# A decoder trunk with its five engines in program order, weight splits two tiles ahead

## The chip, the cores and the metric

The kernel runs on one core of one Trainium2 chip, in one launch. Its time is the device time of that core in microseconds (us), the median of several runs. Five engines work side by side and meet at semaphores: TensorE (PE) multiplies matrices, VectorE (DVE), ScalarE (ACT) and GpSimd (POOL) work element by element, SyncE (SP) issues transfers. Each takes its own instructions in the order in which they are written into its program.

## The reference, cut to what matters

Two layers over 256 tokens of width 1024, in float32, then a final RMSNorm:

```python
h = rmsnorm(x, norm_mix[l])
p = h @ w_in[l]
a_x, a_c, a_b, q, k, v, g, z, gates = split(p)
y_a = short_conv_mixer(a_x, a_c, a_b, conv_w[l]) @ w_a_out[l]
r = retention(rotary(q), rotary(k), v, ret_gn[l])
y_b = (silu(g) * r) @ w_b_out[l]
y_c = spatial_gating(gelu(z), sg_ln[l], sg_w[l], sg_b[l]) @ w_c_out[l]
g_a, g_b, g_c = split(sigmoid(gates), 3)
x = x + (g_a * y_a + g_b * y_b + g_c * y_c) @ w_o[l]
h = rmsnorm(x, norm_xa[l]); mm = rmsnorm(mem, norm_mem[l])
x = x + cross_attention(h, mm, xa_q[l], xa_k[l], xa_v[l], xa_o[l])   # 4 heads of 256
h = rmsnorm(x, norm_ffn[l])
x = x + (silu(h @ w1[l]) * (h @ w3[l])) @ w2[l]                       # width 2816
```

## The kernel before

Activations lie transposed in SBUF (features on the partitions, 256 tokens along the free side), so a product with a weight takes K tiles of 128 features. To come near float32 with TensorE's fp32r type, every operand is a pair hi + lo, where hi is the value rounded to fp32r and lo the rest, and a product is three: hi·hi, hi·lo and lo·hi. On PE a K tile of 128x128 weights is one matmul of hi against [x hi, x lo] (512 columns) and one of lo against x hi (256 columns).

All weights form one stream, `ws`, of 320 tiles of 128x1024 (512 KB), in the order in which PE wants them. A tile of most stages holds four K tiles of 256 output columns, so a chunk of 256 columns over K = 1024 takes two tiles. `fetch()` does three things with a tile: it issues the transfer into `raw` (five buffers) on SP's queue, lets ACT round it to `hi` (line 106) and DVE subtract to `lo` (both four buffers). `weights()` hands PE the next columns and calls `fetch()` for AHEAD = 1 tile ahead.

The stages of a layer: q/k and v together, z, g, then ax, ac, ab (the convolution's factors), twelve chunks of gates (gt), the three branches' outputs (y) with their gated merge (ye, mg), the first quarter of the keys (k), wo, the other keys, q, the values (xv) with the four heads' attention between (s, pT, av), xo, the FFN's f chunks, w2. In wo, xo and w2 every chunk ends in `residual()`, which adds the PSUM chunk to `xT` in two DVE additions, and `prepare()`, which splits the new `xT` into `xs` for the next stage (ACT makes the hi part with the gain, DVE the lo part, for two blocks) and lets POOL square and sum it into an accumulator (sq, acc). For gates and f chunks the sum of the two PSUM halves is made by `summed()` (a copy by ACT, an addition by DVE), gated by DVE or POOL with the row of norms (rb), and passed on. A gate chunk goes on to ACT's sigmoid into gs. During the gates, the memory tokens (`m2`, from `memT`) are loaded, squared (first layer), scaled on POOL and split into `mmt` for the keys.

What sets the order: only PE's instructions are bound to the order in which the program writes them, by the class `InOrder` (line 36), which gives every instruction a dependency on the one before it on that engine. Those of DVE, ACT, POOL and SP are placed by the framework's scheduler, which runs a timeline model of its own when the program is built, and may take a later tile's split ahead of a written earlier instruction.

Of the kernel before, what the change touches and what calls it, by code (L numbers as in the profile page):

```python
# [17 lines left out]
P = 128  # L18
# [8 lines left out]
LAYER_COLS = 163840  # L27
NPAR = 48
WARM = 9
AHEAD = 1  # L30

IN = dict(ax=0, ac=256, ab=512, q=768, k=1024, v=1280, g=1792, z=2304, gates=2816)

# [20 lines left out]
@with_exitstack  # L54
def decoder_trunk(ctx: ExitStack, tc: tile.TileContext, a, out):
    nc = tc.nc
    V, A, G, T = nc.vector, nc.scalar, nc.gpsimd, InOrder(tc, nc.tensor)

    const = ctx.enter_context(tc.tile_pool(name="const", bufs=1))
    res = ctx.enter_context(tc.tile_pool(name="res", bufs=1))  # L60
# [5 lines left out]
    def tt(e, o, x, y, op):  # L66
        e.tensor_tensor(o, x, y, op=op)  # L67
# [18 lines left out]
        at = sum(m for _, _, m in pieces[-1])  # L86
        pieces[-1].append((at, c, n))
    assert len(pieces) == tiles
    state = dict(pos=0, loaded=0)
    ready = []  # L90
    later = []

    def fetch():
        n = state["loaded"]
        if n == tiles:
            return
        state["loaded"] = n + 1
        raw = wts.tile([P, TW], F32, tag="raw", name=f"raw{n}", bufs=5)
        hi = wts.tile([P, TW], F32R, tag="hi", name=f"hi{n}", bufs=4)
        lo = wts.tile([P, TW], F32R, tag="lo", name=f"lo{n}", bufs=4)  # L100
        for at, c, m in pieces[n]:
            nc.sync.dma_start(raw[:, at:at + m], ws[c // TW, :, c % TW:c % TW + m])
        w = TW if n else TW // 2
        for c in range(0, TW, w):
            sl = slice(c, c + w)
            A.activation(hi[:, sl], raw[:, sl], AF.Copy)  # L106
            tt(V, lo[:, sl], raw[:, sl], f32(hi[:, sl]), ALU.subtract)
        if n >= 4 and later:
            later.pop(0)()
        ready.append((hi, lo))  # L110

    def weights(cols):
        pos = state["pos"]
        while state["loaded"] <= min(pos // TW + AHEAD, tiles - 1):
            fetch()
        o = pos % TW
        state["pos"] = pos + cols
        hi, lo = ready[pos // TW]
        return hi[:, o:o + cols], lo[:, o:o + cols]


    def chunk_T(xs, kt, name, hooks=None, ps=None, ks=None):


# [12 lines left out]
        return ps  # L137
# [85 lines left out]
    sgg = const.tile([P, L, 256], F32, name="sgg")  # L223
    gfin = const.tile([P, KT], F32, name="gfin")
    for t, n in ((cs, "cs"), (dec, "dec"), (tril, "tril"), (gfin, "gfin")):
        later.append(lambda t=t, n=n: nc.sync.dma_start(t, a[n]))
    later.append(lambda: nc.sync.dma_start(sgg, a["sgg"].partition_broadcast(P)))

    def param(l, name):
        o, n = dict(g_mix=(0, 8), g_xa=(8, 8), g_mem=(16, 8), g_ffn=(24, 8), gn=(32, 4),  # L230
# [50 lines left out]
    def new_acc(name):  # L281
        return wrk.tile([P, S], F32, tag="acc", name=name, bufs=2)
# [14 lines left out]

    acc = new_acc("acc0")
    for j in range(4):
        nc.sync.dma_start(xT[:, 2 * j:2 * j + 2], a["xT"][:, 2 * j:2 * j + 2])  # L300
        prepare(j, acc, param(0, "g_mix"))
        for _ in range((2, 1, 1, 0)[j]):
            fetch()
    rm = const.tile([P, S], F32, name="rm")

    for l in range(L):
# [38 lines left out]


        wm = wrk.tile([P, 4, P], F32, tag="wm", name="wm", bufs=1)
        nc.sync.dma_start(wm, a["wsT"][:, l])
        tt(G, wm, wm, mid(tril, 4), ALU.mult)
        st6 = wrk.tile([P, 2, 6], F32, tag="st6", name="st6")  # L350
        mv2 = wrk.tile([P, 2, 2], F32, tag="mv2", name="mv2")
# [50 lines left out]
        for i in range(2):
            V.tensor_scalar_mul(yc[:, i], zp[:, i, 2:], cw[:, 4 + i:5 + i])
            V.scalar_tensor_tensor(yc[:, i], zp[:, i, 1:S + 1], cw[:, 2 + i:3 + i], yc[:, i], ALU.mult, ALU.add)
            V.scalar_tensor_tensor(yc[:, i], zp[:, i, 0:S], cw[:, i:i + 1], yc[:, i], ALU.mult, ALU.add)
# [20 lines left out]
        for b in range(2):  # L426
# [4 lines left out]
            rv = rr[:, b].rearrange("p h d -> p (h d)")  # L431
            tt(G, rv, rv, sg[:, b], ALU.mult)

        tb = summed(chunk_T(of(xs), KT, f"ab{l}"))
        tt(G, tb, tb, mid(rb, 2), ALU.mult)
        tt(G, yc, yc, tb, ALU.mult)
        split(mo[:, 0:2], yc)
        split(mo[:, 6:8], transposes(su, 0, f"suT{l}"))


# [1 line left out]
        for c in range(12):  # L442
            t = summed(chunk_T(of(xs), KT, f"gt{l}_{c}"))
            tt(V, t, t, mid(rb, 2), ALU.mult)
            A.activation(gs[:, 2 * c:2 * c + 2], t, AF.Sigmoid)
            if c == 2 and l == 0:
                macc = new_acc("macc")
                for j in range(4):
                    m2 = wrk.tile([P, 2, S], F32, tag="pp", name="m2", bufs=2)
                    nc.sync.dma_start(m2, a["memT"][:, 2 * j:2 * j + 2])  # L450
                    add_squares(macc, m2, j == 0)
            if c == 5 and l == 0:
                rm_n = rstd_cols([macc], "rm_n")
# [32 lines left out]
        kv = wrk.tile([P, 8, 2, S], F32R, tag="A", name=f"kT{l}", bufs=1)
# [129 lines left out]
        if l + 1 < L:
# [114 lines left out]
```

## Time and profile before

| | |
|---|---|
| runs | 968.21, 968.31, 970.08 us; median 968.31 |
| the profiled execution | 969.4 us |
| its span (first to last instruction) | 967.6 us |
| mean granted clock of PE | 0.995 |
| instructions | 14606 |
| moved by DMA | 175.53 MB, 181 GB/s in the mean |

The span is 1.8 us shorter than the execution's time. "Busy" is the sum of an engine's instructions; a wait is put down to the semaphore that came last. The granted clock is PE's, 1.00 being full speed. Tile names in a row stand for all tiles of that name.

### The profile page before, as it was taken

How to read it: one execution, taken by the hardware profiler on the slowest of the kernel's cores; microseconds unless marked ns; L12 is line 12 of the kernel's file. 1: busy time of each engine (PE TensorE's matmuls, PEld its weight loads, DVE VectorE, ACT ScalarE, POOL GpSimd, SP SyncE). 2: the span in 40 equal slices, each digit the busy share in tenths (PEclk: the TensorE clock that was granted, in tenths of full speed). 3: DMA queues.
4: the chain of work that ended last, by engine and by line, in shares of the span. 5: the costliest groups of instructions: out<-in, count | busy, mean ns of one | idle time of the engine just before them, and what ended most of it. 6: DMA issues, size and time to landing. Idle time of an engine off the chain costs nothing.

```text
span 967.6 us, 14606 instructions
## 1 busy us (share of the span) xinstructions
PE 951.8 (98%) x5622; PEld 836.8 (86%) x5622; DVE 713.7 (74%) x884; ACT 539.8 (56%) x740; POOL 296.1 (31%) x232
## 2 busy tenths in 40 slices
PE   8999999999999999999999989999999999999996
PEld 6788889888998888888888878998889888888886
DVE  7679789886768866657655896799776778666654
ACT  6565765565645755654456465545665466656431
POOL 5943021320114644432134230024100345444211
PEclk9999999999999999999999999999999999999998
DMA  9664665555546565555656355555644556556541
GB/s 310 245 228 145 192 203 186 190 182 170 172 133 194 177 198 191 193 187 180 197 179 194 111 180 193 195 179 172 196 153 151 154 187 191 187 194 194 180 151 44
DMA packets 52630, 175.53 MB, mean 181 GB/s; under 512 B 6096, under 2 KB 6608, under 8 KB 52560
## 3 DMA queue, kind: packets, MB, share of 16 engines
q1 hardware_dynamic: 52128, 174.03, 55.9%
q8 instruction: 44, 0.72, 0.3%
q10 hardware_dynamic: 432, 0.57, 0.2%
q14 instruction: 26, 0.21, 0.1%
HBM read 173.53 MB, written 1.05 MB: 180 GB/s over the span
## 4 chain that ended last, share of the span: by engine, by line
PE 96%; DVE 2%; DMA 1%; issue 0%; SPq 0%; ACT 0%; DVEq 0%
PE f L43 25%; PE gt L43 14%; PE w L43 13%; PE y L43 5%; PE k L43 5%; PE xo L43 5%; PE wo L43 5%; PE xv L43 5%; PE q L43 5%; PE z L43 2%; PE g L43 2%; PE v L43 2%; PE qk L43 2%; PE av L43 1%; PE ac L43 1%; PE s L43 1%
## 5 line engine op out<-in xcount | busy, mean ns | idle before, releaser
L67 DVE TENSOR_TENSOR lo<-raw,hi 128x1024 fp32r<-128x1024 f32 (+1 forms) x321 | 436.8, 1363 | 200.0 <-ACT hi L106 198.0
L106 ACT ACTIVATE hi<-raw 128x1024 fp32r<-128x1024 f32 (+1 forms) x321 | 338.9, 1057 | 315.1 <-issue 67.5
L43 PE MATMUL f<-xs,hi 128*128 128x512 f32 x704 | 245.2, 393 | 0.0
L43 PE MATMUL f<-xs,lo 128*128 128x256 f32 x704 | 196.1, 279 | 0.0
L43 PEld LDWEIGHTS f<-xs,hi 128*128 128x128 f32 x704 | 131.9, 187 | 30.1 <-issue 0.4
L43 PE MATMUL gt<-xs,hi 128*128 128x512 f32 x384 | 136.5, 400 | 2.8 <-DVE ev L67 2.7
L43 PEld LDWEIGHTS f<-xs,lo 128*128 128x128 f32 x704 | 132.6, 188 | 0.0
L67 POOL TENSOR_TENSOR sq<-xT 128x512 f32<-128x512 f32 x27 | 45.8, 1695 | 239.3 <-DVE xT L67 234.5
L43 PE MATMUL gt<-xs,lo 128*128 128x256 f32 x384 | 107.8, 281 | 0.0
L67 POOL TENSOR_TENSOR ev<-ev,rb_ffn 128x512 f32<-128x512 f32 x44 | 63.8, 1453 | 108.3 <-DVE ev L67 85.3
L43 PEld LDWEIGHTS gt<-xs,hi 128*128 128x128 f32 x384 | 72.7, 189 | 20.6 <-DVE ev L67 4.0
L43 PEld LDWEIGHTS gt<-xs,lo 128*128 128x128 f32 x384 | 73.2, 191 | 0.0
L43 PE MATMUL w<-aB,hi 128*128 128x512 f32 (+1 forms) x198 | 62.7, 372 | 0.0
L43 PE MATMUL w<-aA,hi 128*128 128x512 f32 (+1 forms) x198 | 62.3, 371 | 0.0
L67 POOL TENSOR_TENSOR ev<-ev 128x256 f32<-128x256 f32 x44 | 50.5, 1151 | 20.1 <-ACT ev L597 20.1
L202 DVE SCALAR_TENSOR_TENSOR xs<-xT,par,xs 128x256 fp32r<-128x256 f32 x48 | 49.1, 1062 | 4.2 <-ACT xs L201 4.2
L43 PE MATMUL w<-aB,lo 128*128 128x256 f32 x176 | 49.5, 281 | 0.0
L43 PE MATMUL w<-aA,lo 128*128 128x256 f32 x176 | 49.4, 281 | 0.0
L43 PE MATMUL y<-mo,hi 128*128 128x256 f32 x256 | 46.1, 283 | 0.0
L43 PE MATMUL k<-mmt,hi 128*128 128x512 f32 x128 | 45.6, 400 | 0.0
L43 PE MATMUL q<-xs,hi 128*128 128x512 f32 x128 | 45.5, 398 | 0.0
L43 PE MATMUL xo<-ox,hi 128*128 128x512 f32 x128 | 45.4, 399 | 0.0
(251 smaller groups left out, 1779.9 us busy)
## 6 DMA issues: line engine op xcount, KB each, us to landing
raw<-in_ws SPq DMA_DIRECT2D x304, 512.0 KB, 3.5
raw<-in_ws SPq DMA_DIRECT2D x32, 256.0 KB, 4.0
m<-in_memT SPq DMA_DIRECT2D x12, 256.0 KB, 4.0
xT<-in_xT SPq DMA_DIRECT2D x4, 256.0 KB, 5.2
dec<-in_dec SPq DMA_DIRECT2D x1, 512.0 KB, 6.0
wm<-in_wsT SPq DMA_DIRECT2D x2, 256.0 KB, 4.8
out<-xT ACTq DMA_DIRECT2D x2, 256.0 KB, 2.3
sgg<-in_sgg SPq DMA_DIRECT2D x1, 256.0 KB, 5.1
```

Source lines behind the costliest of these rows:

```text
L43: ins = getattr(self.engine, name)(*args, **kwargs)
L67: e.tensor_tensor(o, x, y, op=op)
L106: A.activation(hi[:, sl], raw[:, sl], AF.Copy)
L202: V.scalar_tensor_tensor(lo, x, scale, f32(hi), ALU.mult, ALU.subtract)
```

## The change

All five engines become `InOrder`, so no scheduler moves an instruction. The program itself is written as a pipeline instead. `fetch()` is cut in two: `load()` issues the transfer and runs LOADED = 4 tiles ahead of the split, `cut()` makes hi and lo and is called when PE begins the tile AHEAD = 2 before. Work that waits for a POOL result is handed to `after(units, fn)`, which lets `weights()` call it so many K tiles (UNIT = 256 columns) later: the convolution's taps (3), its split (6), the memory's split (7), the merge of the branches (2), the FFN's gate (4) and hidden split (6). The memory tokens' squares are spread over gate chunks 2 to 5, and the tokens scaled in chunks 7 to 10 in place of 6 to 9. At the start all blocks of x and the first five weight tiles are issued to SP before the first `prepare()`. The computation is the same.

```diff
-AHEAD = 1
+AHEAD = 2
+LOADED = 4
+UNIT = 256
-    V, A, G, T = nc.vector, nc.scalar, nc.gpsimd, InOrder(tc, nc.tensor)
+    V, A, G, T, Y = (InOrder(tc, e) for e in (nc.vector, nc.scalar, nc.gpsimd, nc.tensor, nc.sync))
-    def fetch():
-        n = state["loaded"]
...
+    def load():
+        n = len(raws)
...
+        for at, c, m in pieces[n]:
+            Y.dma_start(raw[:, at:at + m], ws[c // TW, :, c % TW:c % TW + m])
+        raws.append(raw)
+    def cut():
+        n = len(ready)
...
+        while len(raws) <= n:
+            load()
...
+        if n >= 4:
+            while len(raws) <= min(n + LOADED, tiles - 1):
+                load()
...
+    def after(units, fn):
+        due.append((state["unit"] + units, fn))
     def weights(cols):
         pos = state["pos"]
-        while state["loaded"] <= min(pos // TW + AHEAD, tiles - 1):
-            fetch()
+        while len(ready) <= min(pos // TW + AHEAD, tiles - 1):
+            cut()
...
+        state["unit"] = pos // UNIT
+        for item in [d for d in due if d[0] <= state["unit"]]:
+            due.remove(item)
+            item[1]()
...
+                def memory(j=j, m2=m2):
+                    for n in range(2):
+                        split(mmt[:, 2 * j + n], m2[:, n], param(l, "g_mem")[:, 2 * j + n:2 * j + n + 1])
+                after(7, memory)
...
-            tt(V, ev[0], ev[0], ev[2], ALU.add)
-            split(mg[:, 2 * c:2 * c + 2], ev[0])
+            def merge(c=c, ev=ev):
+                tt(V, ev[0], ev[0], ev[2], ALU.add)
+                split(mg[:, 2 * c:2 * c + 2], ev[0])
+            after(2, merge)
...
-            A.activation(t[:, 0], t[:, 0], AF.Silu)
-            tt(G, t[:, 0], t[:, 0], t[:, 1], ALU.mult)
-            split(hidden(c), t[:, 0])
+            def gate():
+                A.activation(t[:, 0], t[:, 0], AF.Silu)
+                tt(G, t[:, 0], t[:, 0], t[:, 1], ALU.mult)
+            after(4, gate)
+            after(6, lambda: split(hidden(c), t[:, 0]))
```

In order rows, `lo60` is weight tile 60's lo part and the number behind an underscore tells two buffers apart; wo0_1 is layer 0's second chunk of wo. First DVE in wo of the first layer. Before:

```order
L67 TENSOR_TENSOR lo60_1864<-raw60_1862,hi60_1863 128x1024
L67 TENSOR_TENSOR kT0_1733<-ev_1779,kT0_1733 128x2x256
L67 TENSOR_TENSOR xT_73<-wo0_0_1785,xT_73 128x512 x2
L67 TENSOR_TENSOR lo61_1897<-raw61_1895,hi61_1896 128x1024
L202 SCALAR_TENSOR_TENSOR xs_74<-xT_73,par_75,xs_74 128x256 x2
L67 TENSOR_TENSOR lo62_1919<-raw62_1917,hi62_1918 128x1024
L67 TENSOR_TENSOR xT_73<-wo0_1_1839,xT_73 128x512 x2
L67 TENSOR_TENSOR lo63_1952<-raw63_1950,hi63_1951 128x1024
L202 SCALAR_TENSOR_TENSOR xs_74<-xT_73,par_75,xs_74 128x256 x2
```

After, DVE there reads:

```order
L45 TENSOR_TENSOR lo58_1801<-raw58_1676,hi58_1800 128x1024
L45 TENSOR_TENSOR lo59_1823<-raw59_1712,hi59_1822 128x1024
L45 TENSOR_TENSOR xT_73<-wo0_0_1799,xT_73 128x512 x2
L45 SCALAR_TENSOR_TENSOR xs_74<-xT_73,par_75,xs_74 128x256 x2
L45 TENSOR_TENSOR lo60_1855<-raw60_1750,hi60_1854 128x1024
L45 TENSOR_TENSOR lo61_1877<-raw61_1775,hi61_1876 128x1024
L45 TENSOR_TENSOR xT_73<-wo0_1_1853,xT_73 128x512 x2
L45 SCALAR_TENSOR_TENSOR xs_74<-xT_73,par_75,xs_74 128x256 x2
```

Between the additions to xT and the two operations on xs stood one split, and stands none; at wo's first addition the splits are done up to tile 60 before, up to tile 59 after.

DVE in xo of the first layer, whose first two chunks end one weight tile apart. Before:

```order
L67 TENSOR_TENSOR xT_73<-xo0_0_2737,xT_73 128x512 x2
L67 TENSOR_TENSOR lo92_2887<-raw92_2885,hi92_2886 128x1024
L202 SCALAR_TENSOR_TENSOR xs_74<-xT_73,par_75,xs_74 128x256 x2
L67 TENSOR_TENSOR xT_73<-xo0_1_2775,xT_73 128x512
L67 TENSOR_TENSOR lo93_2920<-raw93_2918,hi93_2919 128x1024
L67 TENSOR_TENSOR xT_73<-xo0_1_2775,xT_73 128x512
L67 TENSOR_TENSOR lo94_2942<-raw94_2940,hi94_2941 128x1024
L202 SCALAR_TENSOR_TENSOR xs_74<-xT_73,par_75,xs_74 128x256 x2
```

After:

```order
L45 TENSOR_TENSOR lo90_2814<-raw90_2663,hi90_2813 128x1024
L45 TENSOR_TENSOR xT_73<-xo0_0_2751,xT_73 128x512 x2
L45 SCALAR_TENSOR_TENSOR xs_74<-xT_73,par_75,xs_74 128x256 x2
L45 TENSOR_TENSOR lo91_2845<-raw91_2708,hi91_2844 128x1024
L45 TENSOR_TENSOR xT_73<-xo0_1_2789,xT_73 128x512 x2
L45 SCALAR_TENSOR_TENSOR xs_74<-xT_73,par_75,xs_74 128x256 x2
L45 TENSOR_TENSOR lo92_2878<-raw92_2756,hi92_2877 128x1024
```

Before, splits 92, 93 and 94 stand ahead of the second chunk's xs; after, only split 91 does, and both chunks' xT and xs are ahead of split 92.

ACT at the gates of the second layer, where m2_5769 and m2_5826 are pieces of the memory tokens and gt1_1 is the second gate chunk. Before:

```order
L190 ACTIVATE ev_5331<-gt1_0_5286 128x512
L198 ACTIVATE mo1_4686<-mixb1_4684 128x2x256
L106 ACTIVATE hi188_5428<-raw188_5427 128x1024
L106 ACTIVATE hi189_5456<-raw189_5455 128x1024
L190 ACTIVATE ev_5381<-gt1_1_5336 128x512
L201 ACTIVATE mo1_4686<-rT10_5386,par_75 128x256
L201 ACTIVATE mmt1_5654<-m2_5769,par_75 128x256 x2
L201 ACTIVATE mo1_4686<-rT12_5395,par_75 128x256
L445 ACT_TABLE_LOAD
L445 ACTIVATE gs1_5285<-ev_5331 128x512
L201 ACTIVATE mmt1_5654<-m2_5826,par_75 128x256 x2
L106 ACTIVATE hi190_5478<-raw190_5477 128x1024
```

After, the first piece of the memory tokens (m2_5719) comes here:

```order
L45 ACTIVATE ev_5663<-gt1_6_5618 128x512
L45 ACTIVATE gs1_5297<-ev_5663 128x512
L45 ACTIVATE hi198_5670<-raw198_5573 128x1024
L45 ACTIVATE hi199_5692<-raw199_5595 128x1024
L45 ACTIVATE ev_5714<-gt1_7_5669 128x512
L45 ACTIVATE gs1_5297<-ev_5714 128x512
L45 ACTIVATE hi200_5723<-raw200_5623 128x1024
L45 ACTIVATE hi201_5745<-raw201_5645 128x1024
L45 ACTIVATE mmt1_5668<-m2_5719,par_75 128x256 x2
```

The splits of the memory tokens stood among those of the first two gate chunks; they now stand behind the eighth gate chunk's sigmoid.

## Rows read from the trace of the kernel before

**Rows 1.** The page's busy time: us, share of span, instructions of each engine.

```profile
PE 951.8 (98%) x5622; PEld 836.8 (86%) x5622; DVE 713.7 (74%) x884; ACT 539.8 (56%) x740; POOL 296.1 (31%) x232
```

**Rows 2.** The chain that ended last: start, us, engine, tile, line, instructions.

```profile
91.22 22.19 PE gt L43 x128
147.36 23.03 PE y L43 x192
176.04 22.62 PE wo L43 x128
```

**Rows 3.** PE's waits: releaser, us in total, times, longest us.

```profile
PE gt L43 <- DVE ev L67: 2.7, 3, 2.1
PE qk L43 <- DVE lo L67: 2.0, 3, 0.7
PE rb_fin L43 <- DVE rn_fin L259: 1.3, 1, 1.3
PE qk L43 <- ACT hi L106: 0.9, 1, 0.9
PE rb_mix_ps L43 <- DVE rn_mix L259: 0.7, 1, 0.7
```

**Rows 4.** Timeline, second layer's gates: start, us, engine, line, operation, tile [idle before].

```profile
564.44 4.93 POOL L67 TENSOR_TENSOR m<-m,rm 128x512 f32<-128x512 f32 x2 [4.19 <-DMA m<-in_memT]
568.13 0.91 ACT L201 ACTIVATE mmt<-m,par 128x256 fp32r<-128x256 f32 x2 [3.69 <-POOL m L67]
577.19 0.50 PE L43 MATMUL gt<-xs,hi 128*128 128x512 f32 x1 [2.11 <-DVE ev L67]
```

**Rows 5.** Windows: the start, and behind that wait: busy us, clock, DMA share, GB/s.

```profile
5.50:32.00 26.50, 23.24 (x99) 17.72 (x100) 21.71 (x24) 15.25 (x22) 17.81 (x17) 1.00 1.00 352
578.40:581.90 3.50, 3.50 (x14) 2.94 (x13) 2.90 (x4) 0.97 (x2) 0.00 (x0) 0.51 0.78 256
```

**Rows 6.** Timeline of DVE, ACT and POOL in wo, first layer.

```profile
181.74 1.42 DVE L67 TENSOR_TENSOR xT<-wo,xT 128x512 f32<-128x512 f32 x2
183.07 1.22 DVE L67 TENSOR_TENSOR lo<-raw,hi 128x1024 fp32r<-128x1024 f32 x1
183.19 0.91 ACT L201 ACTIVATE xs<-xT,par 128x256 fp32r<-128x256 f32 x2 [0.46 <-DVE xT L67]
183.24 1.95 POOL L67 TENSOR_TENSOR sq<-xT 128x512 f32<-128x512 f32 x1 [11.05 <-DVE xT L67]
184.20 2.14 DVE L202 SCALAR_TENSOR_TENSOR xs<-xT,par,xs 128x256 fp32r<-128x256 f32 x2
186.27 1.21 DVE L67 TENSOR_TENSOR lo<-raw,hi 128x1024 fp32r<-128x1024 f32 x1
187.41 1.41 DVE L67 TENSOR_TENSOR xT<-wo,xT 128x512 f32<-128x512 f32 x2
191.93 1.76 DVE L67 TENSOR_TENSOR lo<-raw,hi 128x1024 fp32r<-128x1024 f32 x1
```

**Rows 7.** Groups by form: busy us, mean ns | idle before us and releaser.

```profile
L202 DVE SCALAR_TENSOR_TENSOR xs<-xT,par,xs 128x256 fp32r<-128x256 f32 x48 | 49.1, 1062 | 4.2 <-ACT xs L201 4.2
L198 ACT ACTIVATE mg<-ye 128x512 fp32r<-128x512 f32 x8 | 5.0, 628 | 0.8 <-DVE ye L67 0.7
L523 DVE TENSOR_REDUCE mx<-s 128x2 f32<-128x512 f32 x8 | 5.5, 684 | 0.0
L528 ACT ACTIVATE pp<-s,mx,rs 128x256 f32<-128x256 f32 x16 | 8.8, 557 | 5.5 <-DVE mx L67 5.5
L530 DVE RECIPROCAL sm<-sm 128x2 f32<-128x2 f32 x8 | 1.3, 164 | 9.2 <-ACT pp L528 9.2
```

**Rows 8.** Timeline: the same operation on m, POOL idle, second layer.

```profile
571.77 0.89 DVE L202 SCALAR_TENSOR_TENSOR mmt<-m,par,mmt 128x256 fp32r<-128x256 f32 x2 [0.73 <-ACT mmt L201]
```

**Rows 9.** Timeline: DVE in the y stage, first layer.

```profile
164.57 0.68 DVE L67 TENSOR_TENSOR mg<-ye,mg 128x512 fp32r<-128x512 f32 x1
165.17 0.68 DVE L67 TENSOR_TENSOR ye<-y,gs 128x512 f32<-128x512 f32 x1
```

More of the change, by code (lines that the diff above doesn't have):

```diff
@@ L88, in decoder_trunk @@
     assert len(pieces) == tiles
-    state = dict(pos=0, loaded=0)
-    ready = []
-    later = []
-    def fetch():
-        n = state["loaded"]
+    state = dict(pos=0, loaded=0, unit=0)
+    raws, ready = [], []
+    later, due = [], []
+    def load():
+        n = len(raws)
         if n == tiles:
             return
-        state["loaded"] = n + 1
         raw = wts.tile([P, TW], F32, tag="raw", name=f"raw{n}", bufs=5)
+        for at, c, m in pieces[n]:
[3 more added lines that the diff above has]
+        n = len(ready)
+        if n == tiles:
+            return
+        while len(raws) <= n:
+            load()
+        raw = raws[n]
         hi = wts.tile([P, TW], F32R, tag="hi", name=f"hi{n}", bufs=4)
         lo = wts.tile([P, TW], F32R, tag="lo", name=f"lo{n}", bufs=4)
-        for at, c, m in pieces[n]:
-            nc.sync.dma_start(raw[:, at:at + m], ws[c // TW, :, c % TW:c % TW + m])
         w = TW if n else TW // 2
@@ L107, in fetch @@
             tt(V, lo[:, sl], raw[:, sl], f32(hi[:, sl]), ALU.subtract)
-        if n >= 4 and later:
-            later.pop(0)()
         ready.append((hi, lo))
+        if n >= 4:
+            while len(raws) <= min(n + LOADED, tiles - 1):
+                load()
+            if later:
+                later.pop(0)()
+    def after(units, fn):
+        due.append((state["unit"] + units, fn))
     def weights(cols):
         pos = state["pos"]
-        while state["loaded"] <= min(pos // TW + AHEAD, tiles - 1):
-            fetch()
+        while len(ready) <= min(pos // TW + AHEAD, tiles - 1):
+            cut()
         o = pos % TW
         state["pos"] = pos + cols
+        state["unit"] = pos // UNIT
+        for item in [d for d in due if d[0] <= state["unit"]]:
+            due.remove(item)
+            item[1]()
         hi, lo = ready[pos // TW]
@@ L225, in decoder_trunk @@
     for t, n in ((cs, "cs"), (dec, "dec"), (tril, "tril"), (gfin, "gfin")):
-        later.append(lambda t=t, n=n: nc.sync.dma_start(t, a[n]))
-    later.append(lambda: nc.sync.dma_start(sgg, a["sgg"].partition_broadcast(P)))
+        later.append(lambda t=t, n=n: Y.dma_start(t, a[n]))
+    later.append(lambda: Y.dma_start(sgg, a["sgg"].partition_broadcast(P)))
     def param(l, name):
@@ L299, in decoder_trunk @@
     for j in range(4):
-        nc.sync.dma_start(xT[:, 2 * j:2 * j + 2], a["xT"][:, 2 * j:2 * j + 2])
+        Y.dma_start(xT[:, 2 * j:2 * j + 2], a["xT"][:, 2 * j:2 * j + 2])
+        for _ in range((2, 1, 1, 1)[j]):
+            load()
+    for j in range(4):
         prepare(j, acc, param(0, "g_mix"))
         for _ in range((2, 1, 1, 0)[j]):
-            fetch()
+            cut()
     rm = const.tile([P, S], F32, name="rm")
@@ L347, in decoder_trunk @@
         wm = wrk.tile([P, 4, P], F32, tag="wm", name="wm", bufs=1)
-        nc.sync.dma_start(wm, a["wsT"][:, l])
+        Y.dma_start(wm, a["wsT"][:, l])
         tt(G, wm, wm, mid(tril, 4), ALU.mult)
@@ L401, in decoder_trunk, with taps @@
         cw = param(l, "conv")
[L402 to L405, printed above, removed]
+        def taps():
+            for i in range(2):
+                V.tensor_scalar_mul(yc[:, i], zp[:, i, 2:], cw[:, 4 + i:5 + i])
+                V.scalar_tensor_tensor(yc[:, i], zp[:, i, 1:S + 1], cw[:, 2 + i:3 + i], yc[:, i], ALU.mult, ALU.add)
+                V.scalar_tensor_tensor(yc[:, i], zp[:, i, 0:S], cw[:, i:i + 1], yc[:, i], ALU.mult, ALU.add)
         rr = mb[:, 0:2].rearrange("p b (h d) -> p b h d", h=4)
@@ L432, in decoder_trunk @@
             tt(G, rv, rv, sg[:, b], ALU.mult)
+        after(3, taps)
         tb = summed(chunk_T(of(xs), KT, f"ab{l}"))
@@ L436, in decoder_trunk @@
         tt(G, yc, yc, tb, ALU.mult)
-        split(mo[:, 0:2], yc)
+        after(6, lambda: split(mo[:, 0:2], yc))
         split(mo[:, 6:8], transposes(su, 0, f"suT{l}"))
@@ L445, in decoder_trunk @@
             A.activation(gs[:, 2 * c:2 * c + 2], t, AF.Sigmoid)
[L446 to L453, printed above, removed]
+            if l == 0 and 2 <= c < 6:
+                if c == 2:
+                    macc = new_acc("macc")
+                m2 = wrk.tile([P, 2, S], F32, tag="pp", name="m2", bufs=2)
+                Y.dma_start(m2, a["memT"][:, 2 * (c - 2):2 * (c - 2) + 2])
+                add_squares(macc, m2, c == 2)
             if c == 6:
                 if l == 0:
-                    rows_kept(rm_n, "rm", rm)
+                    rm_n = rstd_cols([macc], "rm_n")
                 mmt = wrk.tile([P, KT, 2, S], F32R, tag="M", name=f"mmt{l}", bufs=1)
-            if 6 <= c < 10:
-                j = c - 6
+            if c == 7 and l == 0:
+                rows_kept(rm_n, "rm", rm)
+            if 7 <= c < 11:
+                j = c - 7
                 m2 = wrk.tile([P, 2, S], F32, tag="pp", name="m2", bufs=2)
-                nc.sync.dma_start(m2, a["memT"][:, 2 * j:2 * j + 2])
+                Y.dma_start(m2, a["memT"][:, 2 * j:2 * j + 2])
                 tt(G, m2, m2, mid(rm, 2), ALU.mult)
-                for n in range(2):
-                    split(mmt[:, 2 * j + n], m2[:, n], param(l, "g_mem")[:, 2 * j + n:2 * j + n + 1])
+                def memory(j=j, m2=m2):
+                    for n in range(2):
+                        split(mmt[:, 2 * j + n], m2[:, n], param(l, "g_mem")[:, 2 * j + n:2 * j + n + 1])
+                after(7, memory)
             if c == 1:
@@ L610, in decoder_trunk @@
             if c >= 3:
-                while len(ts) > 1:
+                for _ in range(min(2, len(ts))):
                     gated(ts.pop(0), c - len(ts))
-        gated(ts[0], FT - 1)
         acc = new_acc(f"acc_out{l}")
@@ L643, in decoder_trunk @@
                 V.scalar_tensor_tensor(xT[:, n], xT[:, n], gfin[:, n:n + 1], rp, ALU.mult, ALU.mult)
-        (nc.sync if i % 2 == 0 else A).dma_start(out[:, n0:n1], xT[:, n0:n1])
+        (Y if i % 2 == 0 else A).dma_start(out[:, n0:n1], xT[:, n0:n1])
 def _tables():
```

## The prediction

> **What bounds the kernel now.** I read the busy line of the page first. TensorE (PE) is busy 98% of the span, VectorE (DVE) 74%, ScalarE (ACT) 56%, GpSimd (POOL) 31% [rows 1]. The chain of waits shows what a stage costs when nothing is missing: 22.62 us for wo's 128 matmuls, 0.353 for a hi and lo pair, so 5.66 us for each of its four column chunks and 2.83 us for each of its eight weight tiles [rows 2]. The table of PE's waits then gives everything it lost: 2.7 us on DVE's gate evacuations in three waits, the longest 2.1; 2.9 us at the start on the splits for the first q/k tiles; 0.7 us on rn_mix; the rest in the tail [rows 3]. A saving can only come out of this list. A loss can come from every tile split or activation that DVE delivers later than now.
>
> I read the one long wait backwards. POOL waits 4.19 us for a piece of memory, m, until 564.44, and holds it for 4.93 us in two pieces. ACT stands for 3.69 us in front of its split of m at 568.13, with weight splits queued behind, so the gates' evacuation is late and PE starts at 577.19 after 2.11 us idle [rows 4]. Then the granted clock is 0.51 for 3.5 us, PE's lower level (1.2 GHz), and that before is 1.00 [rows 5]. The 14 matmuls of that window, two of them cut by its edges, are 6 to 7 pairs, which take 2.1 to 2.5 us at 0.353: another 1.0 to 1.4 us went there, and I take 1.2.
>
> **What the change gains.** With five engines in program order and the split of m put off by seven K tiles, ACT evaluates the gates first and comes to m later; in the new order the split of a piece stands behind eight evacuated chunks. I count as gone: 2.1 us, the 1.2 us of low clock behind it, 0.6 us of the other two gate waits, and 0.7 us on rn_mix (the squares in the first layer start earlier, all loads being issued ahead) [rows 3 to 5]. Sum 4.6 us. The waits on the first q/k tiles stay, since DVE's order is the same there: the loads are earlier, but DVE still has prepare() of two blocks ahead of each split. What the tail waits for is not moved. PE's own order is the same but for one column of rm, so nothing else changes by itself.
>
> **What it costs: the residual of wo.** In the order of before, the scheduler puts one weight split between the two residual additions (xT) and the two operations for xs, and runs three tiles ahead: tiles 60 and 61 are split by then. After, DVE does xT, xT, xs, xs without a split between, and only up to tile 59 is ready. Now xs needs ACT's first half, which can start only after xT. One round on DVE in the new order, in us from start to start, by [rows 6]:
> - xT x2: 181.74 to 183.07, 1.33.
> - wait for ACT's first xs, which starts 183.19 and takes 0.46: until 183.65, so 0.58, and 0.07 for the handover: 0.65. Before, the split at 183.07 lay in this hole.
> - xs x2: 184.20 to 186.27, 2.07.
> - the first split behind it, beside POOL's sums, by the one at 191.93: 1.7.
> - the second: 186.27 to 187.41, 1.14.
>
> Sum 6.89 against 5.66 of PE, so DVE falls 1.23 behind in every chunk. Until now the same work took 5.67 (181.74 to 187.41) because the hole was filled, and the tile lead took up the rest. PE, with tiles 58 and 59 in hand for 5.66, needs tile 60 when DVE has spent 1.33 + 0.65 + 2.07 + 1.7 = 5.75: 0.1 late. The next three are late by 1.23 each. In front of it the y stage already leaves DVE behind: its round is one clean split 1.14, a contended one 1.7, three products and two sums at 0.60 from start to start, and a wait for ACT's half of mg (0.63 and handover), which nothing fills now: 6.6 against 23.03/4 = 5.76 [rows 2, 7, 9]. 0.85 of that lag comes out at wo. The hi product runs first, which forgives 0.23 of a late lo. So 0.1 + 3 x 1.23 + 0.85 - 0.23 = 4.4 per layer.
>
> **The residual of xo.** There the first two residuals stand only one tile apart, so DVE does two groups of xT and xs with one split between: tile 92 is ready 5.75 + 5.75 = 11.5 after the first one starts, where PE needs it at 5.75 + 2.83 = 8.6, so 2.9. The later two are 1.2 and 1.25, as in wo, the first 0.1; less 0.23, 5.2 per layer.
>
> **The smaller places**, per layer. Attention: DVE takes for each head the maximum (0.68), waits for ACT's two exponentials (2 x 0.56), then takes the reciprocal (0.16) and scales, about 3.2 with the handovers, an estimate. The reciprocal's wait, 9.2 us in 8 times, is there already [rows 7], but in the order of before splits fill part of the time around it and run further ahead; four heads, their other pieces and the splits make about 30.2 of DVE between the last q chunk but one and tile 82, against 29.2 of PE, so 1.05 late. z to g 0.3, sc to vm 0.4 (an evacuation of ax is now ahead of it), and the statistics and taps in front of the first gate 0.9 (estimates, from the additions counted there at 0.60 and splits at 1.14 against 2.83 for a tile). That makes 4.4 + 5.2 + 1.05 + 1.6 = 12.25, two layers 24.5, and 0.5 once at the end of w2: 25. In the FFN's steady chunks and the gates I cost the change at nothing: DVE has two splits (2.3 to 3.4), one addition and one product at 0.60 [rows 9], below the 5.55 us of a gate chunk (22.19/4) [rows 2]. This cover is PE's own work; a DVE round has to grow by 1.5 us before a chunk pays anything.
>
> **Bounds.** The weak term is xs, of which no row shows the new neighbours. At the slow end it is the 2.07, with both splits contended: 7.4 per round, 0.5 more, ten such rounds: +6. At the fast end xs goes as the same operation goes beside an idle POOL, 0.89 for two [rows 8]; then the round is 1.33 + 0.65 + 0.9 + 1.14 + 1.14 = 5.2 and nothing is lost in wo, while xo's pair loses about 0.6. I take the slow xs, because POOL squares xT right behind xT in both kernels. The new places of y, attention and the small ones may cost from 0 to 6 per layer; I keep 3.4.
>
> The row at 183.24 is worth a look: sq takes 1.95 there beside a split that started before it, at 183.07, and the split kept its 1.13 [rows 6]. The Trainium skill, "SBUF — State Buffer", section "Who interferes with whom", says that VectorE and GpSimd share a port pair, and that whichever starts first holds it for a whole instruction while the other stands. By this rule sq goes first after the change, because no split starts before it, and xs stands until sq and the sums leave it: a round of 6.5 to 6.8 instead of 6.89, a sum 2 to 3 us smaller, the same sign.
>
> **The sum** for the profiled execution: span 967.6 - 4.6 + 25 = 988.0. Around the span are 1.8 us, which gives 989.8; this execution (969.4) was 1.1 above the median of the runs, 968.31, so the time for a median is 988.7, say 988.5.
>
> **Rivals.**
> 1. The clock drops again and again (chance 0.17). For it: after a gap of 2.11 the clock fell to 0.51 for 3.5 us [rows 4, 5]. Against: the gaps on the first q/k tiles, 0.7 to 0.9, had none of this (clock 1.00 there), and most new gaps lie between, at 1.2 [rows 3, 5]. Where DVE is the bound, a slower PE only fills its next wait; the 1.2 us count where a row of gaps ends: wo, xo and attention, two layers, 6 x 1.2 = 7: 996. [...]
> 2. The other side: faster (0.13). POOL and DVE don't meet, since POOL is idle 69% of the span and put off by the change; xs at 0.9 gives the round of 5.2 above, below 5.66. Then only the gain of 4.6 and about 1 of small losses: 965. It decides at a round of 5.66, that is when xs takes under 1.35 for two. Against: xs has a mean of 1.06 over 48 [rows 7], so the slow one is the rule.
> 3. Half the loss (0.10): the small places and y cost nothing, and xo and wo go with a round of 6.3 (0.65 x 6 + 2.9 + 0.2 = about 7 per layer): 968.3 - 4.6 + 14 = 978.
> 4. Nothing to be seen (0.05): gains and losses cancel, or DVE's wait is shorter than 0.65 because ACT gets at xT by halves: 968.
>
> The forecast keeps 0.55. Its own range is 980 to 994. For 8 in 10 I take 970 to 1001: that leaves out rival 2 and 4, and nearly nothing above. Two kernels that differ by less than 0.2% (1.9 us) can't be told apart here, so faster is 0.13, the same 0.05, slower 0.82.
>
> **What would show it.** PE's table of waits after the change: waits of wo and xo on lo, some 1.2 us each and one near 2.9 per layer in xo, together 19; the wait of gt on ev gone and the clock at 1.00 around it. DVE in wo: xs directly behind xT with an idle of 0.6 ahead of it named ACT xs, and lo at intervals that come to 6.9 per chunk. If PE's waits on lo stay under 5 us in all, the round was shorter than I take it, and rival 2 or 3 holds; if PE's busy time grows by over 5 us with the clock at half, rival 1.

## The result: 1028 us, three times the loss that was forecast

The changed kernel takes 1027.96 us (median, 1025.28 to 1028.87) against 969.19 for the one before on the same chip: a ratio of 1.060 (95% interval 1.058 to 1.062). It is slower, as forecast, but by 59 us, not 20, and outside the range of 970 to 1001. The line of busy times and the chain that ended last, by engine, on the page of the changed kernel:

```profile
PE 978.5 (95%) x5622; PEld 840.6 (82%) x5622; DVE 703.3 (68%) x884; ACT 521.6 (51%) x740; POOL 292.8 (29%) x232
...
PE 42%; DVE 29%; ACT 10%; issue 9%; POOL 7%; DMA 2%; SPq 0%; DVEq 0%; ACTq 0%
```

Before, PE was 98% busy [rows 1], and the page's line of the chain was:

```profile
PE 96%; DVE 2%; DMA 1%; issue 0%; SPq 0%; ACT 0%; DVEq 0%
```

Now PE is 42% of the chain, which runs through DVE, ACT and POOL as well. PE's table of waits (releaser, us in total, times, longest):

```profile
PE gt L45 <- DVE lo L45: 8.8, 13, 1.7
PE k L45 <- DVE lo L45: 3.1, 6, 0.6
PE xo L45 <- DVE lo L45: 3.1, 2, 1.6
PE rm_n_ps L45 <- POOL macc L45: 3.0, 1, 3.0
PE f L45 <- DVE lo L45: 2.9, 6, 0.6
PE wo L45 <- DVE lo L45: 2.9, 6, 0.6
...
PE gt L45 <- ACT hi L45: 2.5, 2, 1.3
PE y L45 <- DVE ye L45: 2.3, 4, 1.1
```

The wait that the change was to take away, gt on ev [rows 3], is gone, and gt now waits 11.3 us on weight splits. The table shows too little of f: 2.9 us, where the stage grew by 14.7. A lo that comes 0.1 us late at every tile falls below what it lists. So the sum is better read by stage, from the first matmul of a stage to the first of the next (us, both layers; the rows make 57.7 of the 59.1 us between the two spans):

| stage | before | after | more | forecast, more |
|---|---|---|---|---|
| gates (gt) | 141.8 | 161.8 | 20.0 | -2.1 |
| branch outputs (y) | 46.1 | 52.4 | 6.3 | 0 (lag shown in wo) |
| keys and wo | 91.4 | 100.7 | 9.3 | 8.8 |
| xv with attention | 61.9 | 65.7 | 3.8 | 2.1 |
| xo | 48.1 | 51.7 | 3.6 | 10.4, with f's start |
| f | 245.9 | 260.7 | 14.7 | 0 |

Two stages whose steady chunks were forecast at no cost, gates and f, make 35 of the 59 us.

**The f stage.** ACT, DVE and POOL in two f chunks of the changed kernel, from three timelines (ev<-ev by ACT is the Silu):

```profile
401.23 0.42 ACT L45 ACTIVATE ev<-ev 128x256 f32<-128x256 f32 x1 [2.76 <-POOL ev L45]
401.56 1.04 ACT L45 ACTIVATE hi<-raw 128x1024 fp32r<-128x1024 f32 x1
...
407.10 0.42 ACT L45 ACTIVATE ev<-ev 128x256 f32<-128x256 f32 x1 [2.75 <-POOL ev L45]
```

```profile
402.63 1.22 DVE L45 TENSOR_TENSOR lo<-raw,hi 128x1024 fp32r<-128x1024 f32 x1 [2.58 <-ACT hi L45]
403.78 0.42 DVE L45 TENSOR_TENSOR aB<-ev,aB 128x256 fp32r<-128x256 f32 x1
404.11 0.68 DVE L45 TENSOR_TENSOR ev<-f,ev 128x512 f32<-128x512 f32 x1
404.71 1.22 DVE L45 TENSOR_TENSOR lo<-raw,hi 128x1024 fp32r<-128x1024 f32 x1
```

```profile
399.00 2.20 POOL L45 TENSOR_TENSOR ev<-ev,rb_ffn 128x512 f32<-128x512 f32 x1 [2.41 <-DVE ev L45]
...
404.87 2.20 POOL L45 TENSOR_TENSOR ev<-ev,rb_ffn 128x512 f32<-128x512 f32 x1 [2.40 <-DVE ev L45]
```

They are a ring. The Silu (401.23) waits for POOL; hi stands behind it in ACT's order (401.56); lo waits for that hi (402.63); the sum of the next chunk's halves stands behind lo in DVE's order (404.11); POOL's product waits for the sum (404.87); the next Silu waits for POOL (407.10). One round is 407.10 - 401.23 = 5.87 us, longer than PE's 5.55 to 5.66 for a chunk, so PE gets its lo just too late, chunk after chunk. POOL's product takes 2.20 us in it, where it took 1.45 in the mean before:

```profile
L67 POOL TENSOR_TENSOR ev<-ev,rb_ffn 128x512 f32<-128x512 f32 x44 | 63.8, 1453 | 108.3 <-DVE ev L67 85.3 <-ACT rb_ffn L272 22.9
```

The lo at 404.71 starts 0.16 ahead of it. The Trainium skill, "SBUF — State Buffer", section "Who interferes with whom", has whichever of VectorE and GpSimd starts first hold their port pair; the trace agrees, and in e2 below with the sides changed. With the 1.30 us that POOL's product takes there, this ring would close in about 5.0 us, below PE's chunk; that is an estimate.

**The gates.** Chunks of the first layer, ACT, then DVE:

```profile
90.94 0.63 ACT L45 ACTIVATE gs<-ev 128x512 f32<-128x512 f32 x1 [0.60 <-DVE ev L45]
96.28 0.63 ACT L45 ACTIVATE gs<-ev 128x512 f32<-128x512 f32 x1 [2.33 <-DVE ev L45]
...
110.60 0.63 ACT L45 ACTIVATE gs<-ev 128x512 f32<-128x512 f32 x1 [2.39 <-DVE ev L45]
111.14 2.00 ACT L45 ACTIVATE hi<-raw 128x1024 fp32r<-128x1024 f32 x2
113.16 0.60 ACT L45 ACTIVATE ev<-gt 128x512 f32<-128x512 f32 x1
116.53 0.63 ACT L45 ACTIVATE gs<-ev 128x512 f32<-128x512 f32 x1 [2.77 <-DVE ev L45]
...
122.71 0.63 ACT L45 ACTIVATE gs<-ev 128x512 f32<-128x512 f32 x1 [2.94 <-DVE ev L45]
```

```profile
106.03 3.21 DVE L45 TENSOR_TENSOR lo<-raw,hi 128x1024 fp32r<-128x1024 f32 x2 [1.65 <-ACT hi L45]
109.16 0.68 DVE L45 TENSOR_TENSOR ev<-gt,ev 128x512 f32<-128x512 f32 x1
109.88 0.69 DVE L45 TENSOR_TENSOR ev<-ev,rb_mix 128x512 f32<-128x512 f32 x1
112.21 2.95 DVE L45 TENSOR_TENSOR lo<-raw,hi 128x1024 fp32r<-128x1024 f32 x2 [1.65 <-ACT hi L45]
```

The sigmoid (110.60) waits 2.39 for DVE's product, with both hi behind it; DVE waits 1.65 for them at 112.21, with the next sum and product behind the two lo. The round is 116.53 - 110.60 = 5.93 and 122.71 - 116.53 = 6.18, against PE's 5.55. In both of them POOL's squares slow the two lo, to 2.95 and 3.21 us, from 2.36. With POOL idle the same round takes 96.28 - 90.94 = 5.34, and in the second layer, which has no squares, it keeps to PE's pace at 5.65 to 5.66 for four chunks. So the gates' round has next to no slack, and what else comes into it PE pays, as far as the lead doesn't cover it: the squares, the parts made from rT (a round of 8.14 in both layers), the splits of the memory tokens (6.1 to 7.2). Then PE waits 3.0 us for POOL's sum of the memory's squares, and its clock falls, as windows show (us, busy of five engines, clock, DMA share, GB/s):

```profile
127.80:134.70 6.90, 6.71 (x22) 5.84 (x23) 4.02 (x9) 4.01 (x5) 0.14 (x1) 0.51 0.46 138
609.10:612.60 3.50, 3.30 (x10) 2.88 (x11) 2.57 (x4) 1.18 (x3) 0.00 (x0) 0.51 0.69 183
```

It is at 0.51, the level of 1.2 GHz, for 6.8 us behind that wait, and for 3.4 us in the second layer, where PE had waited 1.3 us for ACT's hi and 0.8 for lo. Two such waits at the same place in the first layer, 1.2 and 0.8 us at 100.7 and 102.0, left it at 1.00.

**wo**, the round that was worked out ahead, DVE and POOL:

```profile
203.20 1.41 DVE L45 TENSOR_TENSOR xT<-wo,xT 128x512 f32<-128x512 f32 x2
205.19 1.70 DVE L45 SCALAR_TENSOR_TENSOR xs<-xT,par,xs 128x256 fp32r<-128x256 f32 x2 [0.58 <-ACT xs L45]
206.82 2.35 DVE L45 TENSOR_TENSOR lo<-raw,hi 128x1024 fp32r<-128x1024 f32 x2
209.09 1.41 DVE L45 TENSOR_TENSOR xT<-wo,xT 128x512 f32<-128x512 f32 x2
...
215.52 1.41 DVE L45 TENSOR_TENSOR xT<-wo,xT 128x512 f32<-128x512 f32 x2
```

```profile
204.69 1.04 POOL L45 TENSOR_TENSOR sq<-xT 128x512 f32<-128x512 f32 x1 [10.57 <-DVE xT L45]
```

xs stands directly behind xT, with the hole of 0.58 us that names ACT xs. The round is 215.52 - 209.09 = 6.43 (the first one 5.89), the forecast 6.89. sq, ahead of xs now, takes 1.04, not 1.95, and xs 1.63 from start to start, not 2.07 [rows 6].

The kernel before had rounds nearly as long. Only its first took the 5.67 that the forecast compares with; then xT starts at 187.41 [rows 6] and at:

```profile
193.60 1.41 DVE L67 TENSOR_TENSOR xT<-wo,xT 128x512 f32<-128x512 f32 x2
...
199.80 1.40 DVE L67 TENSOR_TENSOR xT<-wo,xT 128x512 f32<-128x512 f32 x2
```

These are rounds of 6.19 and 6.20, and PE lost nothing by them, with splits ready one tile further ahead.

### The profile page after: what moved, and what is told of

Same layout as the page of the kernel before. It is cut to its first block, busy times and chain, and to the rows that moved or that the text cites. A ratio compares the mean times of both kernels' runs of the same rounds, so it can differ in the third digit from the quotient of the medians.

```text
span 1026.7 us, 14672 instructions
## 1 busy us (share of the span) xinstructions
PE 978.5 (95%) x5622; PEld 840.6 (82%) x5622; DVE 703.3 (68%) x884; ACT 521.6 (51%) x740; POOL 292.8 (29%) x232
## 3 DMA queue, kind: packets, MB, share of 16 engines
HBM read 173.53 MB, written 1.05 MB: 170 GB/s over the span
## 4 chain that ended last, share of the span: by engine, by line
PE 42%; DVE 29%; ACT 10%; issue 9%; POOL 7%; DMA 2%; SPq 0%; DVEq 0%; ACTq 0%
DVE lo L45 13%; PE w L45 12%; POOL ev L45 7%; ACT hi L45 6%; PE f L45 5%; DVE ev L45 4%; PE gt L45 4%; PE q L45 3%; DVE xT L45 2%; PE xv L45 2%; PE k L45 2%; PE z L45 2%; DVE ye L45 2%; PE g L45 2%; DVE xs L45 2%
## 5 line engine op out<-in xcount | busy, mean ns | idle before, releaser
L45 DVE TENSOR_TENSOR lo<-raw,hi 128x1024 fp32r<-128x1024 f32 (+1 forms) x321 | 424.8, 1347 | 176.3 <-ACT hi L45 175.3
L45 ACT ACTIVATE hi<-raw 128x1024 fp32r<-128x1024 f32 (+1 forms) x321 | 326.3, 1046 | 43.9 <-PE w L45 31.6
L45 PE MATMUL f<-xs,hi 128*128 128x512 f32 x704 | 249.4, 397 | 0.0
L45 PE MATMUL f<-xs,lo 128*128 128x256 f32 x704 | 201.2, 286 | 3.7 <-DVE lo L45 2.9
L45 PE MATMUL gt<-xs,hi 128*128 128x512 f32 x384 | 140.0, 405 | 2.5 <-ACT hi L45 2.5
L45 POOL TENSOR_TENSOR ev<-ev,rb_ffn 128x512 f32<-128x512 f32 x44 | 92.3, 2102 | 107.0 <-DVE ev L45 79.3
L45 POOL TENSOR_TENSOR sq<-xT 128x512 f32<-128x512 f32 x27 | 30.3, 1121 | 315.9 <-DVE xT L45 310.6
L45 ACT ACTIVATE ev<-ev 128x256 f32<-128x256 f32 x44 | 17.9, 416 | 93.3 <-POOL ev L45 93.3
L45 ACT ACTIVATE xs<-xT,par 128x256 fp32r<-128x256 f32 x48 | 21.8, 502 | 79.3 <-DVE xT L45 77.6
L45 DVE SCALAR_TENSOR_TENSOR xs<-xT,par,xs 128x256 fp32r<-128x256 f32 x48 | 41.1, 896 | 15.5 <-ACT xs L45 15.5
```

The source lines that it names most:

```text
L45: ins = getattr(self.engine, name)(*args, **kwargs)
```

## Experiments

Each ran in three rounds beside the kernel before, which took 970 to 971 us there. The stage times quoted are taken as in the table above.

**e1: the pipeline without the order.**

```diff
-    V, A, G, T, Y = (InOrder(tc, e) for e in (nc.vector, nc.scalar, nc.gpsimd, nc.tensor, nc.sync))
+    V, A, G, T, Y = nc.vector, nc.scalar, nc.gpsimd, InOrder(tc, nc.tensor), nc.sync
```

> The changed program, with only TensorE in program order as before; VectorE, ScalarE, GpSimd and SyncE are free for the scheduler again. Theory 'order' (the loss of 59 us is made where ScalarE and VectorE, now in written order, wait for each other and for GpSimd): back to 960 to 975 us. Rival 'pipeline' (load and cut two ahead, the counts of after() and the moved memory work themselves cost time, whoever orders them): stays above 1000.

Measured 966.74 us, 0.9964 of before (0.9948 to 0.9980). The 'order' theory holds: with the rest of the change in place and only the order taken back, the whole loss goes. It is even a little faster than before, with the lowest median of all kernels here. The second layer's gates take 70.3 us, 72.8 before, and PE's waits of gt on ev, 2.7 us in three times before [rows 3], are:

```profile
PE gt L45 <- DVE ev L69: 0.8, 1, 0.8
```

**e11: the order without the pipeline.** All five engines of the kernel before go in program order, and nothing else:

```diff
-    V, A, G, T = nc.vector, nc.scalar, nc.gpsimd, InOrder(tc, nc.tensor)
+    V, A, G, T, Y = (InOrder(tc, e) for e in (nc.vector, nc.scalar, nc.gpsimd, nc.tensor, nc.sync))
```

> The kernel before with all five engines in written order and nothing else of the change (one tile of lead, loads with the splits, no counts). Theory: order is what costs and the pipeline parts win some of it back, so this is slower than the changed kernel by far: 1060 to 1250. Rival (the pipeline parts bring nothing to a program in order): within 10 us of 1028.

Measured 1294.0 us (1.334, 1.330 to 1.338), beyond the expected band, at a mean granted clock of 0.94 (0.98 to 1.00 in the other kernels), so part of it is the clock's. With e1 the table is whole: neither 969, pipeline alone 967, order alone 1294, both 1028. The pipeline is worth 266 us to a program in order and 3.6 us to a scheduled one.

**e2: open the f ring.**

```diff
-            after(4, gate)
-            after(6, lambda: split(hidden(c), t[:, 0]))
+            after(4 if c < 4 else 8, gate)
+            after(6 if c < 4 else 12, lambda: split(hidden(c), t[:, 0]))
```

> From the fifth f chunk on the FFN's gate is put off by 8 K tiles in place of 4, its split by 12 in place of 6; nothing else. Theory 'ring' (in every f chunk ScalarE's Silu waits for GpSimd, the weight's hi behind it is late, so VectorE's lo, so VectorE's sum, so GpSimd: a round of 5.88 us against 5.6 of TensorE): the f stages go from 130.4 to some 124 us each, 12 to 14 us less in all, 1014 to 1016. Rival 'lead' (splits start too late, two tiles ahead, and any order loses): f stays within 2 us of 130.4 and the time at 1025 to 1029.

Measured 1021.67 us: 6.3 less, f at 126.5 and 126.6. That is between the two expectations, by the time nearer to 'lead' (1025 to 1029), by f nearer to 'ring' (124). The trace shows the ring open. In its f chunks POOL, DVE and ACT read, one timeline each:

```profile
389.17 1.30 POOL L45 TENSOR_TENSOR ev<-ev,rb_ffn 128x512 f32<-128x512 f32 x1 [2.67 <-DVE ev L45]
```

```profile
389.35 2.20 DVE L45 TENSOR_TENSOR lo<-raw,hi 128x1024 fp32r<-128x1024 f32 x1 [0.26 <-ACT hi L45]
```

```profile
390.51 0.42 ACT L45 ACTIVATE ev<-ev 128x256 f32<-128x256 f32 x1
393.43 0.60 ACT L45 ACTIVATE ev<-f 128x512 f32<-128x512 f32 x1 [2.50 <-PE f L45]
```

The Silu waits for nothing; ACT waits for PE, so PE is the bound again. POOL starts 0.18 ahead of lo here, takes 1.30, and it is lo that takes 2.20: the same, with the sides changed. That f isn't back at 123 has two reasons: the first chunks, in which PE still waits 1.1 us per layer for the lo behind xo, and PE's own pace (last section).

**e4: open the gates' ring.**

```diff
-            A.activation(gs[:, 2 * c:2 * c + 2], t, AF.Sigmoid)
+            after(4, lambda t=t, c=c: A.activation(gs[:, 2 * c:2 * c + 2], t, AF.Sigmoid))
```

> The sigmoid of a gate chunk is put off by 4 K tiles, nothing else. Theory 'ring' (the sigmoid on ScalarE waits 2.3 to 3.0 us for VectorE's product with the weight's hi queued behind it, and VectorE's lo waits 1.65 us for that hi): the gates of the first layer go from 84.0 to 76 to 80 us, of the second from 77.8 to 74 to 77; 1017 to 1022. Rival 'lead': within 2 us of 1028.

Measured 1006.89 us: 21 us less from one instruction per chunk, more than expected. Gates 74.3 and 71.6 us, lower than 'ring' has it (76 to 80 and 74 to 77); the surplus is y (23.0 and 23.9, from 26.4 and 26.0), which had inherited the gates' lag, and the wait for the squares, which is 0.7 us in place of 3.0, with no low clock behind it. ACT now has a ready hi on either side of the sigmoid:

```profile
106.25 1.05 ACT L45 ACTIVATE hi<-raw 128x1024 fp32r<-128x1024 f32 x1
107.84 0.63 ACT L45 ACTIVATE gs<-ev 128x512 f32<-128x512 f32 x1 [0.54 <-DVE ev L45]
108.38 1.04 ACT L45 ACTIVATE hi<-raw 128x1024 fp32r<-128x1024 f32 x1
```

**e3: one tile more of lead.**

```diff
-AHEAD = 2
+AHEAD = 3
```

> AHEAD = 3 in place of 2, nothing else. Theory 'ring': a ring's round does not depend on how far ahead the splits are, so the f stages and the first layer's gates stay as they are within 3 us each; only where the lag is passing (y, wo, attention, xo) is half of it absorbed: 1010 to 1020. Rival 'lead': PE's waits on lo and hi go nearly all: 970 to 985.

Measured 1010.79 us, inside the band of 'ring'. f is still 128.6 in both layers: towards its end eight chunks and more in a row take 5.87 to 5.89 us each, the ring's round. wo, xv and xo are back within 0.4 us of before, wo with its rounds of 6.43 unchanged, so what brings wo back is the lead. The keys behind wo stay 1.5 late. The second layer's gates fall to 72.9, which 'ring' had not expected. The first layer's stay (82.8), but by luck: PE's waits for splits there fall too, from 5.5 us to 2.4, and in their place stands

```profile
PE rm_n_ps L45 <- POOL macc L45: 6.9, 1, 6.9
```

with the granted clock at 0.5 for 10.2 us around it. So of the gates' ring e3 shows nothing. y got worse (29.6 and 29.7), where PE waits up to 3.5 us for DVE's ye.

**e12: the residual alone.** In wo, and alike in xo and w2, prepare() is put off by one K tile, which lets a split stand between xT and xs:

```diff
             residual(chunk_T(of(mg), KT, f"wo{l}_{j}"), j)
-            prepare(j, acc, param(l, "g_xa"))
+            after(1, lambda j=j, acc=acc, l=l: prepare(j, acc, param(l, "g_xa")))
```

> The changed kernel with prepare() behind each residual put off by one K tile, so that VectorE has a weight split between xT and xs in wo, xo and w2, and nothing else. The prediction's step (the hole of 0.65 us and the missing split make wo, the keys behind it and xo late): wo, k behind it, xo and the first f chunks lose their excess, 5 to 7 us per layer, 1014 to 1018 in all. Rival (these stages are late from the lag that y leaves, not from their own round): under 4 us in all, 1024 or above.

Measured 1019.87 us: 8.1 less, between the two. Per layer xo won 1.8, and wo, the keys and f 0.6 to 1.0 each. wo stays 1.6 above before. The trace shows why no more came back: with the split in the hole, xs goes back to 2.07 from start to start, and xT starts at

```profile
208.51 1.40 DVE L45 TENSOR_TENSOR xT<-wo,xT 128x512 f32<-128x512 f32 x2
...
214.70 1.40 DVE L45 TENSOR_TENSOR xT<-wo,xT 128x512 f32<-128x512 f32 x2
```

The round is 6.19, as before the change, and still longer than PE's 5.66. What the change took from wo is the lead that covered such rounds, and e3 gives that back. How much of the rest is the lag of y is not shown.

**e6 and e7: one engine free,** the other four in order. e6, and e7 with `V = nc.vector` in its place:

```diff
     V, A, G, T, Y = (InOrder(tc, e) for e in (nc.vector, nc.scalar, nc.gpsimd, nc.tensor, nc.sync))
+    A = nc.scalar
```

> The changed kernel with ScalarE alone handed back to the scheduler, the other four engines in written order. Theory 'ring' (each ring needs ScalarE to hold a ready hi behind a sigmoid, a Silu or a copy that waits): most of the loss goes, 975 to 990. Rival 'VectorE' (what costs is VectorE's own written order, as in wo): 1005 or above.

> The changed kernel with VectorE alone handed back to the scheduler. Theory 'ring': a ring is opened at either engine, but ScalarE still holds hi behind its waits, so less than with ScalarE free: 990 to 1010. Rival 'VectorE': 975 or below, and less than with ScalarE free.

Measured 1035.63 us with ACT free, slower than with none, and 1016.0 with DVE free; f stays at 130 in both. The theory as I had put it fell here: freeing one engine of a ring doesn't shorten f. The rival, VectorE's own order, has the band of e6 right, but it wants 975 or below in e7. Most of what e6 loses against the changed kernel is in g (30.2 us, from 24.0). With ACT free, its order in f is the scheduler's, and that still puts POOL's results ahead of hi:

```profile
381.38 0.42 ACT L636 ACTIVATE ev<-ev 128x256 f32<-128x256 f32 x1 [2.09 <-POOL ev L45]
383.06 0.42 ACT L221 ACTIVATE aA<-ev 128x256 fp32r<-128x256 f32 x1 [1.26 <-POOL ev L45]
383.38 1.05 ACT L118 ACTIVATE hi<-raw 128x1024 fp32r<-128x1024 f32 x1
```

Why the scheduler arranged it so is not shown.

**e5, e8, e9: mend the places and keep the order.** e5 joins the edits of e2, e3 and e4; e8 adds e12's and `after(14, ...)` in place of `after(6, ...)` for the split of yc, for which ACT waits 6.9 us in front of the gates; e9 moves the memory's squares one gate chunk forward. The wait of ACT in the changed kernel, then the two edits:

```profile
87.93 0.63 ACT L45 ACTIVATE mo<-mixb 128x512 fp32r<-128x512 f32 x1 [6.92 <-POOL mixb L45]
```

```diff
-        after(6, lambda: split(mo[:, 0:2], yc))
+        after(14, lambda: split(mo[:, 0:2], yc))
...
-            if l == 0 and 2 <= c < 6:
-                if c == 2:
+            if l == 0 and 1 <= c < 5:
+                if c == 1:
...
```

> The changed kernel with the three edits of the runs before together: AHEAD = 3, the FFN's gate put off by 8 and its split by 12 K tiles, the sigmoid put off by 4. If rings and a short lead are separate causes, their gains add: from 1028 some 21 (sigmoid), 7 (gate) and 12 (lead, in wo, k, xv, xo), so 985 to 990. If they are one cause, the sum gives no more than the best of them and 5: 1000 or above.

> The three edits of e5, and besides the split of yc put off by 14 K tiles in place of 6 and prepare() behind every residual by 1, which puts one weight split between xT and xs on VectorE, as the scheduler of before did. All five engines stay in written order. Theory: it is these five places that cost, not program order as such: 966 to 975. Rival: written order costs by itself, and it stays above 980.

> The kernel of e8 with the squares of the memory tokens in gate chunks 1 to 4 in place of 2 to 5 (first layer only). In e8 PE waits 3.0 us for POOL's sum of these, and its clock is at half for 3.4 us behind it. Theory: both go, the first layer's gates from 74.4 to 69 to 70.5, the time from 975.4 to 970 to 972. Rival (POOL's sums are late because they share SBUF with VectorE, not because the load is late): the wait moves by under 1 us and the time stays above 974.

Measured 981.16, 975.42 and 970.84 us; e8 is 0.4 above its band. The gains add in all: those of e2, e3 and e4 sum to 44.5 us, e5 has 46.8, more than expected. By stage they don't: the gates gain 15.9 in e4 and 6.1 in e3 but 18.4 in e5, and y, which e3 makes 6.9 worse, gains 6.3. So the sum doesn't show that rings and a short lead are separate causes. PE still waits 3.1 and 3.0 us for the squares in e5 and e8. In e9 the first layer's gates went from 74.4 to 69.5, and that wait and the low clock behind it are gone. All five engines stand in program order there, and the ratio to before is 1.0005 (0.9990 to 1.0021): no difference that can be measured. So an order is possible that costs next to nothing; what stood in order behind what, with one tile less of lead, cost 57 us. How much of that is the lead alone, no run shows: e9 has both.

**e10: e9 with only PE in order.**

> The program of e9 with only TensorE in written order, the rest by the scheduler. Theory: what the order costs was the places that are mended in e9, so the scheduler has nothing left to mend: within 4 us of e9, 964 to 972. Rival (the scheduler is worth some us everywhere): 960 or below.

Measured 968.56 us, 0.9979 (0.9964 to 0.9994), within 4 us of e9 as expected. It is 2.3 below e9, by ten runs of each whose ranges overlap (965.8 to 971.6 and 969.3 to 973.6), so a small price of the order may be left. In the two traces f's first layer makes nearly all of the difference, 122.9 us against 125.6, by the two paces of PE in the last section.

## Why the prediction was wrong

- **The step that failed** is "In the FFN's steady chunks and the gates I cost the change at nothing: DVE has two splits ..., below the 5.55 us of a gate chunk." The count of DVE's own work was right, but in written order the round is not one engine's work. It runs through every engine that holds a ready instruction behind a waiting one: 5.87 us over ACT, DVE and POOL in f; in the gates 5.34 over ACT and DVE, and 5.93 to 6.18 beside POOL's squares. I looked for the order's cost only on DVE. e4 and e2 show both rings by opening them: 21 and 6.3 us.
- **wo** came out right in its number: 4.4 per layer forecast, 4.65 measured with the keys on both sides (9.3 in the table), at a round of 6.43 in place of 6.89. That is in part luck. The forecast set the new round against 5.67, but before the change the second and third round took 6.19 and 6.20 and were covered by splits further ahead. Filling the hole (e12) wins 1.9 of the 4.65 back; one tile more of lead (e3) brings wo itself back with the same rounds. The prediction's estimate by the Trainium skill ("SBUF — State Buffer", "Who interferes with whom"), 6.5 to 6.8, was nearer to 6.43. y was forecast to lag by its own round; with e4, which leaves that round as it is, y is back at 23.0 in the first layer, so most of its 3.3 came from the gates.
- **xo** was too high: 5.2 per layer forecast, 1.8 in xo and some 1.5 in f's first chunks measured. Its rows have xs at 1.63, as in wo. PE's waits of wo and xo on lo, for which the prediction had 19 us together and one near 2.9 in each layer's xo, are 6.0, or 12.0 with the keys and f, and the longest is 1.6.
- **Attention** was 1.05, measured 1.9; **the start of the gates** was 0.9, and the first gate chunk alone measured 2.0; there ACT waits 6.9 us for POOL's yc with hi behind it, the same kind of place that I had not looked for.
- **The gain** was there but not kept: e1 shows 2.5 of the 3.3 us that I gave to the second layer's gates. In the changed kernel other gaps take their place and the clock falls there again.
- **Rival 1** was partly true: two falls, 6.8 and 3.4 us long, not one behind each row of gaps, and none in wo or xo, where waits are at most 1.6 us. PE's busy time grew by 26.7 us, over the 5 that the prediction took as the sign of this rival, but ahead of the tail the clock was at half for 10.2 us in place of 3.4, which costs about 3.4 us more, an estimate. Rivals 2 to 4 were wrong.

## What to carry to other kernels

Before engines are put in written order, follow each round of a steady stage through all of them: wherever an instruction that waits stands ahead of a ready one that another engine needs, add both into one round, with the times that they take beside their neighbours, and compare that with the bound, not each engine's own work. Move the waiting instruction back by a fraction of a round: the sigmoid by half a chunk was worth 21 us, while a tile more of lead didn't bring f, whose round is too long, back to its time. With five places mended and a tile more of lead, an order by hand was only even with the scheduler's.

## What the runs showed that I had not expected

PE has two paces for the same instructions. These are windows of 50 us in f with PE busy throughout at a clock of 1.00, of e1's first and second layer:

```profile
340.00:390.00 50.00, 50.00 (x291) 44.10 (x290) 34.12 (x37) 30.08 (x46) 23.13 (x19) 1.00 0.61 191
820.00:870.00 50.00, 50.00 (x285) 43.31 (x284) 32.97 (x35) 29.29 (x45) 22.49 (x18) 1.00 0.57 188
```

291 matmuls against 285. The intervals from one hi and lo pair to the next are 0.347 us in the one and 0.353 us in the other, steady through the f stage (the counts include cut ones at the edges): 2.1 us over the 352 pairs of an f stage. In f the kernel before has 0.347 in both layers, e2 0.353, and e8 has 0.353 in the first and 0.347 in the second. Before shows both paces in one layer too, 0.347 in the gates and 0.353 in wo [rows 2]. What sets it is open.
